# A hybrid decoder layer on one core: shift and squares through PSUM, kept low halves for the input projection, and a place of its own for the last phase's scaled x

## The chip, the core and the metric

The kernel runs on one core of a Trainium2 chip. The metric is device time of one execution in microseconds (us); lower is better. Several executions are timed and their median is given. A separate execution is profiled: its trace tells when each instruction of each engine ran.

The engines have these names in the profile: PE does matrix products (PEld its weight loads), DVE is the vector engine, ACT the scalar engine, POOL the GpSimd engine, SP the engine that issues most DMAs. SBUF and PSUM are the on-chip memories; PSUM receives the matrix products; the kernel divides it into eight banks, m0 to m3, aux0, aux1, cb and dec.

## What is computed

One decoder layer for 1024 prompt rows and 8 sample rows of width 1024, cut to what matters here:

```python
h = x + 0.5 * rmsnorm(swiglu(rmsnorm(x, n_ffn1_pre), gate1, up1, down1), n_ffn1_post)
proj = rmsnorm(h, n_mix_pre) @ w_in                     # 1024 x 3328
q, k, v, pb = ...                                        # attention takes q, k, v; RWKV-7 takes pb
xs = pb + (shifted(pb) - pb) * mu_shift                  # token shift, shifted by one row
r, k, v, xw, xa, xg = split(xs)                          # then decay, delta rule, group norm, gate
h = h + rmsnorm(concat(attention, rwkv) @ w_out, n_mix_post)
h = h + 0.5 * rmsnorm(swiglu(rmsnorm(h, n_ffn2_pre), gate2, up2, down2), n_ffn2_post)
```

The feed-forward blocks have an inner width of 2816. The outputs are h for all rows and the new keys, values, matrix states and shift rows.

## The kernel before

**Tiles and phases.** The rows are cut into two halves: 512 prompt rows with the 8 samples (520 columns), and 512 prompt rows. Activations lie transposed, features on the 128 partitions, rows along the free axis. The stream called trunk does the feed-forward work in four phases: phase 0 and 1 are the first block for the first and the second half, phase 2 and 3 the second block. Phases 0 and 3 use, for most of their gates and ups, a scheme with seven block products in place of eight (`s_combine`, `seven`). Between the phases lie the input projection (stream proj, once per half), the jobs of the RWKV part (four per half), rotary encoding, attention (attn0, attn1), decoding for the samples (dec, decb) and the output projection (out for the first half, outb for the second).

**Precision.** Every float32 product is done as three faster ones: each operand is split into a high part (a rounded copy) and a low part (value minus high part). `split` (L599) does this for weights: a copy on ACT, then a subtraction on DVE or POOL, whichever is free sooner, into one of the buffers w0 to w3. As a weight is used for both halves, the low part may be kept: if `kept` is given, the first use writes the low part to DRAM after it is computed (`aside`, L615) and the second use reads it from there straight into the low half of the buffer, with no subtraction. `LOWS` (L99) names where this is done: the second feed-forward block (1) and w_out ("out"), but not w_in. Which buffer serves which column of w_in is fixed in `s_linear` (L652): columns alternate between two buffers, and a column's buffer is filled once the column before last has been used. `s_project` (L1438) orders the 26 columns of 128 outputs; in the second half 24 of them are computed on all 512 rows at once. A finished column goes to the DRAM tile PT.

**Token shift.** `mixed` (L1627) loads one 128-feature strip of 512 rows, with the row before, from PT into a tile E. It subtracts on POOL and then multiplies by mu_shift and adds on DVE. It is called twice in `s_lora` (L1640) and three times in each of four jobs, per half.

**Norms.** `stats` (L794) takes the sum of squares over eight tiles for a norm: ACT squares a tile, DVE or POOL adds it up. The squares lie in SBUF: in a single buffer "sqs" for the phases 2 and 3 (`s_stats`, L1198), in the two buffers "sq" in the tails of phases 0 and 1 (`s_tail`, L1234). `s_pre` (L1206) makes the split operands x of a phase: multiply by the norm, then scale into the high part on ACT and the low part on DVE. For phase 3 the product with the norm lies in the same two buffers "sq" that the trunk's own sums of squares use.

**What sets the order.** The streams are Python generators that put instructions into per-engine queues. A planner (`run`, L475) walks through time with a cost for each instruction and always issues, per engine, what can start first; among those that can start at the same time it takes the one due first. Due times come from a dry run: `latest` (L564) goes backwards through a planned run and notes for each instruction when it is needed at the latest. `BIAS` (L94) shifts the due times of a stream (trunk2 is the trunk's phase 2, job03 the fourth job of the stream job0, and so on, counted over both halves). `PASSES` (L93) says how many dry runs there are, each with the due times of the one before. The resulting order is written into the program for each engine, SP's DMA queue included, and the engines keep to it: an instruction that waits holds up what is queued behind it on its engine.

**Banks and places.** A stream takes its PSUM banks in turn from a list given with it; the jobs begin on the bank "dec", `s_stats`, `s_pre` and the norms after w_out have the same one, and the tails have "dec" and "aux0". The tile "dreg" (4160 words per partition) is used in turn by the first norm, phase 1's activations, the decoding streams, the second half's attention and the combined blocks of phases 0 and 3.

Of the kernel before, what the change touches and what calls it, by code (L numbers as in the profile page):

```python
# [17 lines left out]
AF = mybir.ActivationFunctionType  # L18
ALU = mybir.AluOpType
# [3 lines left out]
P = 128  # L23
# [6 lines left out]
HS = 512  # L30
# [15 lines left out]
NB = 14  # L46
# [11 lines left out]
def const_table():  # L58
# [11 lines left out]
    for g in range(4):  # L70
        for j in range(8):
# [8 lines left out]
W_DEC = 4160  # L80
# [9 lines left out]
MW = 1  # L90
MARG = 0
SLACK = 0.02
PASSES = 2  # L93
BIAS = {"trunk2": 310, "outn3": -60, "outb0": 30, "pre2": -3, "outn0": -30, "rows0": -30, "job00": -10, "job03": 10, "stats0": 10, "dec0": 10, "wts3": 3, "pre3": -30, "mix1": -60, "lora1": 3, "attn11": 3, "tail2": 3}  # L94
SHIFT = {}
RESAT = 3
GROUPS = {(0, 10): [[0, 1, 2], [3, 4], [5, 6, 7], [8, 9]], (3, 6): [[0, 1, 2], [3], [4, 5]],
          (0, 8): [[0, 1, 2], [3, 4], [5], [6, 7]], (0, 6): [[0, 1, 2], [3], [4, 5]], (3, 4): [[0, 1], [2, 3]], (3, 8): [[0, 1, 2], [3, 4], [5], [6, 7]]}
LOWS = (1, "out")  # L99
STARVE = 1  # L100
HUNGER = 0.1
RB = "dec"
# [25 lines left out]
def col(t):  # L128

    return t + TD * (t >= HS)  # L130
# [79 lines left out]
class Kern:  # L210
# [99 lines left out]
    def put(self, eng, op, fn, a, k):  # L310
# [14 lines left out]
        if o.late is not None:  # L325
            o.late += BIAS.get(st.part, 0) + sum(d for a, b, d in self.shift.get(st.part, ()) if a <= o.key[1] < b)
        self.price(o, op, a, k, outs[0], ins)
# [385 lines left out]
    def columns(self):  # L713

        nc, I = self.nc, self.I
        rows = self.E[:, :P]
        t = self.T(self.const, [P, P], "cols")
        r = 0
        for nm in ("n_ffn1_post", "n_mix_pre", "n_mix_post", "n_ffn2_pre", "n_ffn2_post",
                   "subln", "mu_shift", "w0", "a0", "k_k", "k_a", "r_k", "ln_x_w", "ln_x_b"):  # L720
            a = I[nm]
            if len(a.shape) == 3:
                a = a.rearrange("o h d -> o (h d)")
            k = a.shape[1] // P
            nc.sync.dma_start(rows[r:r + k, :], a[0].rearrange("(k p) -> k p", p=P))
            self.col[nm] = (t, r, k)
            r += k
        yield
        pt = self.ps2()
        nc.tensor.transpose(pt[:, :r], rows[:r], self.ident[:r, :r])  # L730
        nc.vector.tensor_copy(t[:, :r], pt[:, :r])
        for nm, k in (("n_ffn1_post", 0.5), ("n_ffn2_post", 0.5), ("subln", 1.0 - LAM_INIT), ("w0", 0.5), ("a0", 0.5)):
            nc.vector.tensor_scalar(self.vecs(nm), self.vecs(nm), k, None, ALU.mult)
        self.omka = self.T(self.const, [P, 4], "omka")
        nc.vector.tensor_scalar(self.omka, self.vecs("k_a"), -1.0, 1.0, ALU.mult, ALU.add)
        yield
# [57 lines left out]
    def stats(self, src, rb, tmp=("sqs", 1), **kw):  # L794

        for k in range(KT):
            self.square_sum(rb, src[k], k, self.tmp(*tmp, rb.shape[-1]), **kw)
        self.rstd(rb)

    def pair(self, k, src, gain, x):  # L800
# [62 lines left out]
    def s_weights(self):  # L863
# [3 lines left out]
        for ph in range(4):  # L867
# [4 lines left out]
            for n, (kind, f, m0) in enumerate(seq):  # L872
# [26 lines left out]
                kept = None  # L899
                if ph // 2 in LOWS and (kind == "down" or f < FAST[3 * (ph // 2)]):  # L900
                    kept = self.Ld[ph // 2][grp[0]:grp[-1] + 1, :, m0 * P:m0 * P + nm].rearrange("q p m -> p q m") if kind == "down" else \
# [304 lines left out]
    def s_pre(self, ph):  # L1206

        half = ph % 2
        if ph > 1:
            yield ("wait", ("outw", half))  # L1210
        for c, (_, n) in enumerate(CHUNKS[ph]):
            yield ("wait", ("stage", ph, c))
            if ph:
                yield ("wait", ("stats", ph, c))
            if c == 0:
                tiles = self.two(half)
                x = self.x[ph] = self.parts(ph, *tiles)
                self.xt[ph] = [t.rearrange("p (k t) -> p k t", t=520) for t in tiles]
            for k in range(KT):
                src = self.staged[c]  # L1220
                if ph:

                    t = self.tmp("sq", 2, n) if ph == 3 else src[k]
                    self.either("tensor_tensor", t, src[k], self.own[c][2][:, :n], ALU.mult)
                    src = {k: t}
                for step in self.pair(k, src, f"n_ffn{1 + ph // 2}_pre", x[c]):
                    step()
                if k % 4 == 3:
                    yield
            self.signal(("x", ph, c))  # L1230
            yield
        self.signal(("staged", ph))
# [141 lines left out]
    def s_loadx(self, half):  # L1374
# [28 lines left out]
        if half == 0:  # L1403
            yield ("wait", ("loaded", 0, "up", RESAT, None))
        for hf in range(2):
# [32 lines left out]
    def s_project(self, half):  # L1438
# [25 lines left out]
        if half:  # L1464
            units[:4] = [(0, 0), (1, 0), (0, 1), (1, 1)]
        yield from self.linear(("in", half), [self.column(self.I["w_in"], m) for m in ms], units, None, out, places,
                               [(self.Li[m], half == 0) for m in ms] if "in" in LOWS else None)
        self.signal(f"proj{half}")

    def s_out(self, half):  # L1470
# [48 lines left out]
        if half:  # L1519
            yield ("wait", "states")  # L1520
        yield from self.linear(("out", half), src, units, px, out, None, [(self.Lo[i % KT], half == 0) for i in range(len(src))] if "out" in LOWS else None)
        self.signal(("outw", half))
# [16 lines left out]
    def s_mix(self, half):  # L1539

        pool = self.pool
        yield ("wait", "setup")
        for m in (24, 25):
            yield ("wait", ("done", half, m))
        yield ("wait", ("staged", 1 + half))
        self.front = self.stage()
        self.spawn(self.s_lora(pool, half), "lora", 0)
        for i in range(4):
            self.spawn(self.s_job(pool, i, half), f"job{i % 2}", 0, "dec")
        self.sets = []  # L1550
        for j in range(2):
            if half:
                yield ("wait", "proj1")
            self.job_buffers(half, j)
            self.signal(("sets", half, j))
        for what in (f"jobs0_{half}", f"jobs1_{half}", f"rope{half}") + ("dec_b",) * half:
            yield ("wait", what)
        self.a_buffers(pool, half)
        self.spawn(self.s_prepare(pool, half), "prep", 0, "cb")
        for b in range(2):  # L1560
            self.spawn(self.s_attend(pool, half, b), f"attn{b}", 0, f"m{2 + b}", f"aux{b}")
        self.spawn(self.s_finish(pool, half), "fin", 0, "cb")
        if half:
            self.spawn(self.s_states(pool), "states", 2, "cb")
        self.spawn(self.s_out(half), "outb" if half else "out", 0, "m2", "m3")
# [61 lines left out]
    def mixed(self, pool, m, s, out, tag):  # L1627

        nc = self.nc
        t0 = col(s * HS)  # L1630
        E = self.first(tag, 1)
        nc.sync.dma_start(E[:, 1:], self.PT[12 + m][:, t0:t0 + HS])
        if s == 0:
            nc.gpsimd.memset(E[:, 0:1], 0.0)
        else:
            nc.sync.dma_start(E[:, 0:1], self.PT[12 + m][:, HS - 1:HS])
        nc.gpsimd.tensor_tensor(out, E[:, 0:HS], E[:, 1:], ALU.subtract)
        nc.vector.scalar_tensor_tensor(out, out, self.vec("mu_shift", m), E[:, 1:], ALU.mult, ALU.add)

# [297 lines left out]
    def s_decode_a(self):  # L1937
        yield ("wait", "setup")
        yield ("wait", ("staged", 1))
        yield ("wait", ("done", 0, 3))  # L1940
        yield ("wait", "lead")
        yield from self.a_decode()
        self.spawn(self.s_decode_b(), "decb", 1, "dec", ahead=8)

    def s_decode_b(self):
        yield ("wait", "proj0")
        take = self.arena(self.T(self.pool, [P, W_DEC], "dreg"))
        yield from self.b_decode(take, take, take(TD, C))
        self.signal("dec_b")

    def s_states(self, pool):

# [587 lines left out]
def hymba_kernel(ctx, tc, I, O, late=None, dry=False):  # L2540
    K = Kern(ctx, tc, I, O, late, dry)
# [35 lines left out]
    for half in range(2):  # L2577
        K.spawn(K.s_project(half), "proj", 0, "m2", "m3")
        K.spawn(K.s_rope(K.pool, half), "rope", 2)
        K.spawn(K.s_mix(half), "mix", 2)  # L2580
    K.spawn(K.s_decode_a(), "dec", 1, "cb", ahead=24)
    K.run()
    if dry:
        raise Planned(K.predicted, K.latest())
# [40 lines left out]
```

## Time and profile before

| | |
|---|---|
| median of 3 runs | 2302.5 us (2299.95 to 2308.67) |
| profiled execution, its own time | 2294.3 us |
| its span, first to last instruction | 2292.3 us |
| mean granted PE clock | 0.991 |
| moved by DMA | 343.15 MB, mean 150 GB/s |

Nearly all lines in the profile are L317, the helper that records every instruction, so the tiles tell what is what: trunk_m is a product of the trunk in one of its banks, wts_w a split feed-forward weight, lin_w a split weight of w_in or w_out, proj_m a product of the input projection, outb_m one of the second w_out, mix_T and mix_X working tiles of jobs and attention, Lo the DRAM tile of the kept low parts of w_out, Dd a DRAM tile of the decoding. An arrow reads output from inputs. In a row of the timeline the first two numbers are start and length in us, and the bracket at its end gives the engine's idle time before it and what ended that. In a row of a tile's view the three numbers are the shortest, median and longest duration in ns, then the first and last start. In a row of groups the numbers behind the bar are busy time in us and mean ns, then the idle time before and its releasers. In the waits the numbers are us in total, count, and the longest. In the rows of stretches each engine's busy time is followed by its count of instructions.

### The profile page before, as it was taken

Reading aid. Unit: us, or ns where it says so; the run is one execution under the profiler, and the core shown is the slowest. Engines: PE = TensorE matmul, PEld = TensorE weight load, DVE = VectorE, ACT = ScalarE, POOL = GpSimd, SP = SyncE. Lnnn points to the kernel's source line nnn. Section 1 sums busy time; section 2 is a strip of 40 time slices with the busy share of each in tenths; the row PEclk is TensorE's granted clock in tenths of the full one; section 3 lists DMA queues with packets and bytes.
Section 4 is the critical chain, followed back from the end, with each engine's and each line's share of the span. In section 5 each row is a group of like instructions: output and inputs, shape, how many; then the busy total and the mean of one; then the engine's idle time right before and its main releaser. Section 6 shows DMA issues by size and latency. Waiting matters only on the chain. (4 is left out here: it accounts for less than half of the span.)

```text
span 2292.3 us, 42829 instructions
## 1 busy us (share of the span) xinstructions
PE 2228.0 (97%) x15857; PEld 1985.3 (87%) x15857; DVE 1556.5 (68%) x3545; ACT 1078.0 (47%) x2231; POOL 1021.6 (45%) x846
## 2 busy tenths in 40 slices
PE   8999999999999999999899999999999999999998
PEld 7999999799887778988787867777788888999998
DVE  5477988756766687477866367665667356777776
ACT  5433443634354365434552145443665556544444
POOL 3344565534343566356543124333443254544443
PEclk9999999999999999999899999999999999999999
DMA  6423334344334576655679643324745847544543
GB/s 205 132 86 100 102 93 130 104 146 140 109 113 108 170 228 204 218 151 151 194 200 225 169 138 114 111 75 121 205 122 168 273 145 249 148 114 130 148 138 111
DMA packets 476295, 343.15 MB, mean 150 GB/s; under 512 B 82457, under 2 KB 424061, under 8 KB 476088
## 3 DMA queue, kind: packets, MB, share of 16 engines
q1 hardware_dynamic: 475480, 338.82, 50.8%
q8 instruction: 125, 2.05, 0.4%
q0 software_dynamic: 320, 1.08, 0.1%
q14 instruction: 82, 0.67, 0.1%
q10 hardware_dynamic: 288, 0.52, 0.1%
HBM read 278.98 MB, written 61.38 MB: 148 GB/s over the span
## 5 line engine op out<-in xcount | busy, mean ns | idle before, releaser
L317 PE MATMUL trunk_m<-trunk_xl,wts_w 128*128 128x256 f32 (+2 forms) x2700 | 459.4, 321 | 6.9 <-DVE trunk_xl L317 6.2
L317 POOL TENSOR_TENSOR wts_w<-wts_raw,wts_w 128x1024 fp32r<-128x1024 f32 (+2 forms) x162 | 314.4, 1948 | 318.1 <-ACT wts_w L317 279.4
L317 PE MATMUL trunk_m<-pre_X,wts_w 128*128 128x512 f32 (+3 forms) x2400 | 439.9, 335 | 5.7 <-POOL wts_w L317 2.8
L317 PEld LDWEIGHTS trunk_m<-trunk_xl,wts_w 128*128 128x128 f32 x2700 | 382.3, 189 | 42.3 <-DVE trunk_xl L317 7.9
L317 PEld LDWEIGHTS trunk_m<-pre_X,wts_w 128*128 128x128 f32 x2400 | 352.6, 190 | 48.2 <-issue 6.8
L317 PE MATMUL trunk_m<-pre_T,wts_w 128*128 128x512 f32 (+3 forms) x1848 | 362.8, 347 | 5.2 <-DVE trunk_xl L317 2.4
L317 ACT CAST wts_w<-wts_raw 128x1024 fp32r<-128x1024 f32 (+2 forms) x293 | 244.2, 848 | 237.9 <-PE trunk_m L317 162.1
L317 PEld LDWEIGHTS trunk_m<-pre_T,wts_w 128*128 128x128 f32 x1848 | 286.9, 190 | 43.7 <-issue 3.8
L317 DVE TENSOR_TENSOR trunk_xl<-trunk_xl,trunk_m 128x256 f32<-128x256 f32 (+2 forms) x351 | 165.8, 489 | 77.3 <-PE trunk_m L317 76.1
L317 PE MATMUL proj_m<-tail_xl,lin_w 128*128 128x256 f32 (+1 forms) x1248 | 168.5, 290 | 2.3 <-POOL lin_w L317 1.9
L317 PEld LDWEIGHTS proj_m<-tail_xl,lin_w 128*128 128x128 f32 x1248 | 155.6, 190 | 11.3 <-issue 7.0
L317 POOL TENSOR_TENSOR trunk_xl<-trunk_t,trunk_xl 128x512 fp32r<-128x512 f32 (+3 forms) x86 | 94.5, 1100 | 149.9 <-ACT trunk_xl L317 149.7
L317 PE MATMUL proj_m<-tail_T,lin_w 128*128 128x512 f32 (+1 forms) x672 | 153.1, 386 | 4.9 <-ACT tail_T L317 3.8
L317 PEld LDWEIGHTS proj_m<-tail_T,lin_w 128*128 128x128 f32 x672 | 122.6, 192 | 33.2 <-ACT tail_T L317 4.2
L317 DVE TENSOR_TENSOR wts_w<-wts_raw,wts_w 128x1024 fp32r<-128x1024 f32 (+2 forms) x101 | 108.1, 1071 | 35.1 <-ACT wts_w L317 34.4
L317 POOL TENSOR_TENSOR wts_w<-wts_lraw,wts_w 128x512 fp32r<-128x512 f32 x44 | 66.4, 1512 | 53.5 <-ACT wts_w L317 46.9
L317 ACT CAST wts_w<-wts_lraw 128x512 fp32r<-128x512 f32 x94 | 55.9, 617 | 64.7 <-DMA wts_lraw<-in_ffn_down_dram 33.4
L317 POOL TENSOR_TENSOR lin_w<-lin_raw,lin_w 128x1024 fp32r<-128x1024 f32 x19 | 45.9, 2417 | 79.4 <-ACT lin_w L317 69.7
L317 DVE TENSOR_TENSOR trunk_t<-trunk_g,trunk_m 128x512 f32<-128x512 f32 (+2 forms) x75 | 42.1, 562 | 53.4 <-PE trunk_m L317 50.7
L317 POOL TENSOR_TENSOR mix_T<-mix_T 128x512 f32<-128x512 f32 x32 | 38.6, 1207 | 79.2 <-DMA mix_T<-PT 54.6
L317 PE MATMUL trunk_aux<-trunk_xl,wts_w 128*128 128x256 f32 (+1 forms) x516 | 71.5, 283 | 0.0
L317 PE MATMUL trunk_m<-comb_T,wts_w 128*128 128x260 f32 x540 | 69.8, 283 | 0.0
(645 smaller groups left out, 4273.9 us busy)
## 6 DMA issues: line engine op xcount, KB each, us to landing
wts_raw<-in_ffn_gate_dram SPq DMA_DIRECT2D x88, 512.0 KB
wts_raw<-in_ffn_up_dram SPq DMA_DIRECT2D x58, 512.0 KB
wts_raw<-in_ffn_down_dram SPq DMA_DIRECT2D x56, 384.0 KB
wts_raw<-in_ffn_down_dram SPq DMA_DIRECT2D x29, 512.0 KB
lin_raw<-in_w_in_dram SPq DMA_DIRECT2D x26, 512.0 KB
wts_w<-Ld SPq DMA_DIRECT2D x22, 512.0 KB
mix_T<-PT SPq DMA_DIRECT2D x37, 256.0 KB
Ld<-wts_w SPq DMA_DIRECT2D x24, 384.0 KB
```

Source lines behind the costliest of these rows:

```text
L317: o = Op(eng, lambda: fn(*a, **k), st)
```

## The change

It does five things. Token shift (`MIX`): ACT scales the strip by 1 - mu_shift into a PSUM bank, and one DVE instruction multiplies the shifted strip by mu_shift and adds that; POOL has no part in it. The factors 1 - mu_shift are made once in `columns`, and the stream lora is given the bank "dec" for this. Squares (`SQP`): in `stats` the squares after the first go to a PSUM bank and DVE does all sums. Low parts: w_in joins `LOWS`, so its low parts are written to the DRAM tile Li in the first half and read in the second. Phase 3's scaled x: all 16 products lie in the tile "dreg", each in its own columns. Order: `PASSES` is 3 and `BIAS` has other entries. The flag `SWAP` is 0, so what hangs on it (another start of the decoding stream decb) does not take place.

```diff
-PASSES = 2
-BIAS = {"trunk2": 310, "outn3": -60, "outb0": 30, "pre2": -3, "outn0": -30, "rows0": -30, "job00": -10, "job03": 10, "stats0": 10, "dec0": 10, "wts3": 3, "pre3": -30, "mix1": -60, "lora1": 3, "attn11": 3, "tail2": 3}
+PASSES = 3
+BIAS = {"trunk2": 300, "outn3": -60, "outb0": 30, "pre2": -3, "prep1": 3, "job11": 3, "attn11": -10, "job12": 30, "states0": -3}
+SWAP = 0
+MIX = 1
+SQP = 1
-LOWS = (1, "out")
+LOWS = (1, "in", "out")
...
+        self.rest_mu = self.T(self.const, [P, NB], "rmu")
+        nc.vector.tensor_scalar(self.rest_mu, self.vecs("mu_shift"), -1.0, 1.0, ALU.mult, ALU.add)
...
         for k in range(KT):
-            self.square_sum(rb, src[k], k, self.tmp(*tmp, rb.shape[-1]), **kw)
+            if SQP:
+                self.square_sum(rb, src[k], k, self.ps2()[:, :rb.shape[-1]], engines=("vector",))
+            else:
+                self.square_sum(rb, src[k], k, self.tmp(*tmp, rb.shape[-1]), **kw)
...
+                scaled = self.T(self.pool, [P, W_DEC], "dreg") if ph == 3 else None
...
-                    t = self.tmp("sq", 2, n) if ph == 3 else src[k]
+                    t = scaled[:, 2112 * c + n * k:2112 * c + n * k + n] if ph == 3 else src[k]
...
-        self.spawn(self.s_lora(pool, half), "lora", 0)
+        self.spawn(self.s_lora(pool, half), "lora", 0, "dec")
...
+        if MIX:
+            part = self.ps2()
+            nc.scalar.activation(part, E[:, 1:], AF.Copy, scale=self.rest_mu[:, m:m + 1])
+            nc.vector.scalar_tensor_tensor(out, E[:, 0:HS], self.vec("mu_shift", m), part, ALU.mult, ALU.add)
+            return
         nc.gpsimd.tensor_tensor(out, E[:, 0:HS], E[:, 1:], ALU.subtract)
         nc.vector.scalar_tensor_tensor(out, out, self.vec("mu_shift", m), E[:, 1:], ALU.mult, ALU.add)
```

More of the change, by code (lines that the diff above doesn't have):

```diff
@@ L1941, in s_decode_a @@
         yield ("wait", "lead")
+        if SWAP:
+            yield ("wait", "decb")
         yield from self.a_decode()
-        self.spawn(self.s_decode_b(), "decb", 1, "dec", ahead=8)
+        if SWAP:
+            self.signal("dec_b")
+        else:
+            self.spawn(self.s_decode_b(), "decb", 1, "dec", ahead=8)
     def s_decode_b(self):
         yield ("wait", "proj0")
+        if SWAP:
+            yield ("wait", "setup")
+            yield ("wait", "lead")
         take = self.arena(self.T(self.pool, [P, W_DEC], "dreg"))
         yield from self.b_decode(take, take, take(TD, C))
-        self.signal("dec_b")
+        self.signal("decb" if SWAP else "dec_b")
     def s_states(self, pool):
@@ L2581, in hymba_kernel @@
     K.spawn(K.s_decode_a(), "dec", 1, "cb", ahead=24)
+    if SWAP:
+        K.spawn(K.s_decode_b(), "decb", 1, "dec", ahead=8)
     K.run()
```

## The prediction, as put on record before the result

> **What bounds the kernel now.** I read the page first, then the stretches of the run stage by stage.
>
> ```profile
> span 2292.3 us, 42829 instructions
> PE 2228.0 (97%) x15857; PEld 1985.3 (87%) x15857; DVE 1556.5 (68%) x3545; ACT 1078.0 (47%) x2231; POOL 1021.6 (45%) x846
> ```
>
> PE is the bound: it idles for 2292.3 - 2228.0 = 64.3 us in all. The change adds and removes no matrix product, so whatever it gains must come out of these 64.3 us. The busy times by stretch say where they lie. Columns: length, then busy time of PE, PEld, DVE, ACT and POOL, granted clock, DMA share, GB/s.
>
> ```profile
> 0.00:30.00 30.00, 19.31 (x99) 17.00 (x100) 16.04 (x51) 20.16 (x40) 10.74 (x13) 0.89 0.51 157
> 1130.00:1150.00 20.00, 12.13 (x60) 11.28 (x60) 13.52 (x28) 10.56 (x24) 12.39 (x15) 0.66 0.83 259
> 1330.00:1600.00 270.00, 262.03 (x1942) 202.00 (x1942) 184.91 (x557) 131.39 (x274) 97.49 (x69) 1.00 0.42 116
> 1840.00:1930.00 90.00, 80.63 (x545) 75.07 (x546) 52.75 (x94) 48.40 (x88) 42.57 (x51) 0.94 0.52 159
> 1930.00:2270.00 340.00, 340.00 (x2833) 339.95 (x2833) 251.61 (x535) 155.32 (x321) 153.33 (x139) 1.00 0.49 145
> 2270.00:2292.30 22.30, 14.44 (x122) 13.55 (x120) 12.40 (x26) 13.48 (x33) 10.12 (x14) 0.95 0.26 96
> ```
>
> The first 30 us lack 10.7 us of PE and the last 22.3 lack 7.9; nothing in the change reaches these. The long last phase, 1930 to 2270, lacks nothing. That leaves 64.3 - 10.7 - 7.9 = 45.7 us. Of these the change comes near three places: the end of the second phase with the start of the second projection (7.9 in 1130 to 1150), the token jobs beside the third phase (8.0 in 1330 to 1600), and the passage into the last phase (9.4 in 1840 to 1930). So the most that it can win is some 25 us, 1.1%, and each engine's relief counts only where PE waits for that engine.
>
> The profiled execution took 2294.3 us, 2.0 more than its span and 8.2 less than the median of 2302.5. I work out a difference against the 2294.3 and add it to the median.
>
> **Low parts of the second projection.** The first projection still computes the low halves of its weights, and now also writes each (26 writes of 512 KB). The second reads them back instead of computing them. What it stops doing, between 1130 and 1330:
>
> ```profile
> L317 DVE TENSOR_TENSOR lin_w<-lin_lraw,lin_w 128x1024 fp32r<-128x1024 f32 x10 | 12.9, 1287 | 2.7 <-ACT lin_w L317 2.7
> L317 DVE TENSOR_TENSOR lin_w<-lin_LT,lin_w 128x1024 fp32r<-128x1024 f32 x6 | 7.8, 1294 | 1.0 <-ACT lin_w L317 1.0
> L317 POOL TENSOR_TENSOR lin_w<-lin_LT,lin_w 128x1024 fp32r<-128x1024 f32 x7 | 17.1, 2443 | 48.3 <-ACT lin_w L317 46.2 <-DMA decb_dreg<-Dd 2.1
> L317 POOL TENSOR_TENSOR lin_w<-lin_lraw,lin_w 128x1024 fp32r<-128x1024 f32 x2 | 5.1, 2534 | 8.2 <-ACT lin_w L317 8.2
> 1141.14 5.08 PE L317 MATMUL proj_m<-tail_T,lin_w 128*128 128x256 f32 x21 [1.17 <-DVE tail_T L317]
> 1230.26 0.63 PE L317 MATMUL job_dec<-init_ident,mix_T 128*128 128x128 f32 x4 [1.86 <-DVE mix_T L317]
> ```
>
> DVE gets back 12.9 + 7.8 = 20.7 us and POOL 17.1 + 5.1 = 22.2. PE waited there for a crowded DVE once inside the projection, 1.86 us, and 1.17 us before it. I take **-1.9**, between 0 and -3.0.
>
> Against it stand the reads. A column's low half can be fetched only when the column before last has left its weight buffer; the fetch then has the time of one column on PE. The same code path already runs in the second w_out, whose fetches the chain of waits shows (start, length):
>
> ```profile
> 1250.00:1300.00 50.00, 50.00 (x216) 40.22 (x215) 25.27 (x31) 11.35 (x12) 9.92 (x5) 1.00 0.72 189
> 1797.65 6.59 DMA lin_w<-Lo
> 1818.17 6.55 DMA lin_w<-Lo
> 1834.32 7.51 DMA lin_w<-Lo
> PE outb_m L317 <- DMA lin_w<-Lo: 2.6, 3, 2.1
> SPq L317 <- PE outb_m L317: 17.6, 9, 3.4
> ```
>
> A wide projection column is 24 products of 50.00 / 216 = 231 ns, 5.6 us. A fetch of 6.55 to 7.51 us is 1.0 to 1.9 us too long for it; 24 wide columns then cost 24 to 46 us if PE has nothing else. In the second w_out PE had products of the third phase between the columns and lost only 2.6 us over 16 fetches; scaled to 24, that is 3.9. The planner sees such waits coming and can put third-phase products here too. The row of the same code path is nearest: **+3.9**, between 0 and +46. By the Trainium skill, "DMA: Bandwidth & Descriptors", section "Anatomy of one DMA", a transfer costs about 2.0 us plus its bytes over 436 GB/s (a fit stated for the GpSimd path), an estimate of 3.2 us for 512 KB; by it the fetch would fit and the sum would be 3.9 lower, but the 6.55 us above disagree with it under load.
>
> The fetch waits on SP for PE. Queued behind it there are raw weights, result stores and the jobs' loads; SP waited 17.6 us for PE that way in w_out, and a raw weight that slips makes the next column late too. Bandwidth is the other limit:
>
> ```profile
> 1130.00:1140.00 10.00, 3.27 (x11) 2.78 (x11) 7.08 (x15) 4.69 (x10) 5.42 (x7) 0.66 0.94 306
> 1200.00:1330.00 130.00, 127.77 (x556) 101.66 (x554) 65.69 (x95) 27.74 (x31) 33.26 (x18) 1.00 0.73 188
> 1840.00:1850.00 10.00, 8.12 (x52) 7.97 (x53) 3.10 (x5) 3.24 (x7) 2.78 (x4) 0.83 0.98 311
> ```
>
> From 1200 to 1330 the DMA is free for 0.27 x 130 = 35 us; 24 fetches are 12.6 MB, 40 us at the full rate of 311 GB/s. It only just does not fit, which is the ground for the upper end. At 1130 the DMA is at 0.94 and 306 GB/s when the phase's tail waits for its residual; two more fetches of 512 KB ahead of that cost 1.05 MB / 306 = 3.4 us, none if behind: **+1.7**.
>
> The 26 writes fall between 450 and 680. The DMA has room there:
>
> ```profile
> 450.00:680.00 230.00, 225.11 (x2048) 206.68 (x2047) 149.34 (x449) 94.34 (x180) 86.52 (x69) 0.99 0.43 124
> ```
>
> 57% of 230 us is free, and 13.6 MB at 311 GB/s are 44. **0**; without that cover a write is 1.7 us before its weight buffer can be refilled.
>
> **Token shift.** A subtraction on POOL and a multiply-add on DVE become a scaling on ACT into PSUM and a multiply-add on DVE that reads it, 28 times. Nearest rows, the last for a DVE operand in PSUM:
>
> ```profile
> L317 POOL TENSOR_TENSOR mix_T<-mix_T x32: 1035/1043/2037, 481.4 to 1502.9; 128x512 f32<-128x512 f32 x32
> L317 DVE SCALAR_TENSOR_TENSOR mix_T<-mix_T,setup_cols,mix_T x24: 732/746/2905, 483.8 to 1487.1; 128x512 f32<-128x512 f32 x24
> L317 ACT ACTIVATE mix_T<-mix_T,setup_cols 128x512 f32<-128x512 f32 x8 | 5.8, 719 | 9.9 <-DVE mix_T L317 9.9
> 1778.80 0.68 DVE L317 SCALAR_TENSOR_TENSOR trunk_g<-trunk_t,trunk_m 128x512 f32<-128x512 f32 x1
> PE job_dec L317 <- DVE job_hres L317: 4.4, 2, 2.4
> POOL mix_T L317 <- DMA mix_T<-PT: 56.8, 16, 8.0
> ```
>
> One shift goes from 1.04 + 0.75 to 0.72 + 0.68, 0.39 us shorter; 28 make 11 us of the jobs' chains, and ACT gets 20 us more. But between 1330 and 1600 PE lacks only 8.0 us, its other time covered by third-phase products. The largest named wait, 4.4 us, is for DVE work of another job queued ahead. One wait changes its queue: POOL stood 56.8 us, at most 8.0 at a time, until a shift's rows had come from DRAM. ACT now takes that wait, and queued behind it are the casts of weights and the copies out of PSUM that PE waits for; PSUM bank dec, which the jobs' own products use, is held until DVE has read it. ACT is busy 131.39 of 270 us, so the order leaves room. I take **-1.0**, between -4.4 and +8.0, one such wait in full. The 14 complements of the shift factors are one small DVE instruction in the setup, and the branches under SWAP are off: 0.
>
> One row is out of line: the 2905 ns among 746. It ran together with this POOL instruction:
>
> ```profile
> 1215.05 2.44 POOL L317 TENSOR_TENSOR lin_w<-lin_LT,lin_w 128x1024 fp32r<-128x1024 f32 x1
> 1215.13 2.90 DVE L317 SCALAR_TENSOR_TENSOR mix_T<-mix_T,setup_cols,mix_T 128x512 f32<-128x512 f32 x1 [1.49 <-POOL mix_T L317]
> ```
>
> DVE stood until POOL was done, then needed its 0.75. Both edits so far remove such pairs. By the Trainium skill, "SBUF — State Buffer", section "SBUF: two separate sides", DVE with two SBUF inputs and POOL lock each other out for a whole instruction; the trace agrees (2.90 beside 2.44).
>
> **Squares in PSUM, scaled x apart.** In four places (the tails of the first two phases, the norms ahead of the last two) 14 sums of squares each went to POOL or DVE; now all go to DVE with the square in PSUM. The last phase's scaled x takes a place of its own, instead of two buffers shared with the trunk's squares. That place is free: by the first two rows attention last reads it at 1756 and the combined blocks come at 1925.
>
> ```profile
> L317 PE MATMUL attn_aux<-mix_dreg,mix_T x16: 309/351/398, 1622.1 to 1756.0; 128*128 128x320 f32 x4, 128*128 128x384 f32 x4, 128*128 128x448 f32 x4, 128*128 128x512 f32 x4
> L317 ACT CAST comb_dreg<-comb_acc x4: 407/409/411, 1925.2 to 1958.0; 128x260 fp32r<-128x260 f32 x4
> L317 POOL TENSOR_TENSOR bset_bv<-bset_bv,stats_sqs x15: 731/774/1456, 1002.0 to 1884.7; 128x256 f32<-128x256 f32 x9, 128x264 f32<-128x264 f32 x6
> 1874.25 3.19 POOL L317 TENSOR_TENSOR outb_T<-outb_T,outn_hres 128x256 f32<-128x256 f32 x4
> 1877.40 2.34 POOL L317 TENSOR_TENSOR wts_w<-wts_raw,wts_w 128x1024 fp32r<-128x1024 f32 x1
> 1879.79 5.81 PE L317 MATMUL trunk_m<-pre_X,wts_w 128*128 128x256 f32 x34 [2.53 <-POOL wts_w L317]
> 1909.06 4.55 PE L317 MATMUL trunk_m<-trunk_xl,wts_w 128*128 128x256 f32 x35 [1.52 <-DVE trunk_xl L317]
> 1918.20 7.62 PE L317 MATMUL trunk_m<-pre_T,wts_w 128*128 128x264 f32 x48 [1.89 <-ACT trunk_sq L317]
> ```
>
> PE waits 2.53 us for a weight that POOL finishes late, behind residual sums and two sums of squares of 0.77; and 1.89 for a trunk square whose buffer the scaled x shares. I take both, **-4.4**, between 0 and -5.9 with the 1.52.
>
> **Sum.** -1.9 + 3.9 + 1.7 - 1.0 - 4.4 = -1.7 us: the profiled execution would come to 2292.6, the median to 2302.5 - 1.7 = **2300.8**. The changed due times and the third planning pass reorder everything besides; I give them 0 and a bound of +-11, a quarter of the 45.7 us that an order can move. A measurement tells about 0.5% from no change, 11.5 us: the forecast is "the same", its own range 2291 to 2314.
>
> **Rivals.** *The fetches stall the second projection* (slower). From the point where the planner keeps the columns back to back as in 1200 to 1330, each pays 6.55 - 5.6 = 1.0 us: 24 us in place of 3.9, 2321. For it: the DMA is overfull by 5 us there. Against: 2.6 us over 16 fetches in w_out. 0.24. *The freed engines pay at once* (faster): all waits named here go (3.0 + 4.4 + 5.9) with no loss to the fetches, and the clock stays up at 1130, where 0.66 over 12.13 busy us costs 4 more: -17, 2285. For it: DVE and POOL lose 43 us of work there, and the standing seen at 1215 with it. Against: of the 7.9 us at 1130 a row here lays only 1.17 to DVE. 0.26. *The new order decides*: the edits do as said, but gaps appear or vanish elsewhere by 12 or more; 0.05 each way.
>
> **Numbers.** Forecast 0.40, the first rival 0.24, the second 0.26, the order 0.10. Faster 0.26 + 0.05 = 0.31, same 0.40, slower 0.29. The range takes in both rivals with half a bound beyond: 2280 to 2326.
>
> **What would show it.** Right: no subtraction left for lin_w after 1130, fetches from a new DRAM tile of 6 to 7 us, PE waits for them of 2 to 6 us in sum, PE idle near 63. Wrong: PE idle in the second projection above 15 us; or, the other way, the passage into the last phase below 3 us and 1130 to 1150 below 4.

## The result and the profile after

The kernel after takes 2286.2 us (median of 4 runs, 2283.27 to 2289.61); the kernel before took 2301.8 us beside it (4 runs, 2299.95 to 2308.67). The ratio is 0.9935, interval 0.9916 to 0.9955: 15.6 us or 0.65% faster. The forecast was 2300.8 us and "the same"; the time that came is that of the second rival, 2285. It lies inside the whole range (2280 to 2326), below the forecast's own (2291 to 2314).

The profiled execution took 2287.7 us. First its page:

```profile
span 2285.6 us, 42938 instructions
PE 2225.9 (97%) x15857; PEld 1980.1 (87%) x15857; DVE 1501.2 (66%) x3568; ACT 1089.2 (48%) x2239; POOL 959.3 (42%) x792
```

PE does the same 15857 products. Its idle time is 2285.6 - 2225.9 = 59.7 us, 4.6 less than before, and its busy time is 2.1 us less. DVE has lost 55 us of work and POOL 62, and the span shows 6.7 of these 117. The two spans differ by 6.7 us, the medians by 15.6: the profiled execution of before was a quick one, 7.5 us under its median. So stretches of the two profiles can show where time went, but they don't add up to the whole difference.

The same stretches as before, and four more, which are needed below (columns as in the prediction):

```profile
350.00:480.00 130.00, 125.66 (x883) 117.20 (x881) 87.57 (x169) 68.68 (x120) 68.50 (x59) 0.99 0.51 158
480.00:1130.00 650.00, 638.32 (x4484) 546.59 (x4483) 427.29 (x1146) 299.18 (x632) 289.81 (x217) 0.99 0.58 172
1130.00:1150.00 20.00, 18.27 (x142) 17.40 (x142) 15.18 (x31) 16.32 (x26) 14.24 (x14) 1.00 0.92 276
1130.00:1200.00 70.00, 66.67 (x398) 58.45 (x398) 46.52 (x89) 45.47 (x76) 38.37 (x32) 1.00 0.85 265
1200.00:1330.00 130.00, 125.53 (x535) 98.36 (x534) 57.70 (x95) 34.02 (x42) 15.54 (x10) 0.99 1.04 276
1330.00:1600.00 270.00, 267.86 (x1908) 206.53 (x1907) 168.76 (x542) 124.93 (x246) 88.77 (x59) 1.00 0.41 115
1840.00:1930.00 90.00, 81.18 (x622) 75.59 (x621) 57.80 (x112) 60.38 (x113) 47.34 (x63) 0.96 0.76 233
1840.00:2000.00 160.00, 151.18 (x1206) 145.58 (x1205) 105.04 (x211) 95.76 (x193) 78.50 (x97) 0.98 0.67 204
```

In the kernel before, the four stretches that the prediction did not show stand so:

```profile
350.00:480.00 130.00, 121.04 (x817) 111.32 (x816) 94.88 (x156) 64.44 (x117) 69.29 (x65) 0.97 0.41 122
480.00:1130.00 650.00, 643.91 (x4561) 552.50 (x4559) 452.22 (x1137) 298.38 (x630) 316.50 (x240) 1.00 0.54 158
1130.00:1200.00 70.00, 61.80 (x348) 54.11 (x349) 47.84 (x90) 36.46 (x69) 36.26 (x37) 0.90 0.72 207
1840.00:2000.00 160.00, 150.63 (x1129) 145.02 (x1130) 102.08 (x188) 88.36 (x172) 77.08 (x88) 0.97 0.55 169
```

PE gained 9.0 - 4.3 = 4.7 us between 350 and 480 (from the first trunk phase to the second, and the start of the first projection), 8.2 - 3.3 = 4.9 us between 1130 and 1200, and 8.0 - 2.1 = 5.9 us beside the jobs. It lost 5.6 us between 480 and 1130 (6.1 idle before, 11.7 now), so that the first gain was spent again by 1130. It lost 2.2 us in the second projection (2.2 idle before, 4.5 now), where DMA is now full (1.04 for 0.73), and 2.5 between 1600 and 1840 (2.2 and 4.6). So it is chance that the three gains add up to 15.5 us, next to the 15.6 of the medians. The passage into the last phase has not become shorter in idle time (8.8 us for 9.4). How the second projection gets its low halves:

```profile
L320 SPq DMA_DIRECT2D lin_w<-Li x26: 319/599/1842, 1126.5 to 1340.9; - x26
L320 POOL TENSOR_TENSOR lin_w<-lin_raw,lin_w x22: 2361/2393/2992, 444.5 to 653.7; 128x1024 fp32r<-128x1024 f32 x22
L320 DVE TENSOR_TENSOR lin_w<-lin_LT,lin_w x3: 1216/1224/1225, 913.3 to 985.3; 128x1024 fp32r<-128x1024 f32 x3
```

There are 26 fetches between 1126.5 and 1340.9, and the last subtractions for lin_w are those of the first projection and of the first w_out; none is left after 1130. What PE waits for (total, count, longest):

```profile
PE trunk_m L320 <- DVE trunk_xl L320: 5.6, 9, 2.1
PE proj_m L320 <- DMA lin_w<-Li: 4.3, 2, 2.3
PE trunk_m L320 <- POOL wts_w L320: 1.4, 4, 0.8
```

The fetches cost PE two waits and 4.3 us. The chain of waits shows one fetch and the column behind it:

```profile
1239.94 8.02 DMA lin_w<-Li
1248.00 7.38 PE proj_m L320 x24
```

### The profile page after: what moved, and what is told of

Read it like the earlier page. It is cut to its first block, busy times and chain, and to the rows that moved or that the text cites. A ratio compares the mean times of both kernels' runs of the same rounds, so it can differ in the third digit from the quotient of the medians.

```text
span 2285.6 us, 42938 instructions
## 1 busy us (share of the span) xinstructions
PE 2225.9 (97%) x15857; PEld 1980.1 (87%) x15857; DVE 1501.2 (66%) x3568; ACT 1089.2 (48%) x2239; POOL 959.3 (42%) x792
## 3 DMA queue, kind: packets, MB, share of 16 engines
q0 software_dynamic: 320, 1.08, 0.1%
## 4 chain that ended last, share of the span: by engine, by line
PE 62%; DVE 5%; DMA 4%; ACT 2%; issue 1%; SPq 1%; POOL 1%; DVEq 0%; ACTq 0%; POOLq 0%
PE trunk_m L320 35%; PE proj_m L320 7%; PE trunk_aux L320 5%; PE job_aux L320 5%; PE out_m L320 2%; PE attn_m L320 2%; PE outb_m L320 2%; PE attn_aux L320 2%; DMA mix_T<-PT 1%; SPq L320 1%; DVE trunk_xl L320 1%; DVE mix_T L320 1%; PE job_cb L320 1%; PE job_dec L320 1%; DMA lin_w<-Lo 0%
## 5 line engine op out<-in xcount | busy, mean ns | idle before, releaser
L320 POOL TENSOR_TENSOR wts_w<-wts_raw,wts_w 128x1024 fp32r<-128x1024 f32 (+2 forms) x170 | 331.9, 1958 | 468.0 <-ACT wts_w L320 352.6
L320 DVE TENSOR_TENSOR wts_w<-wts_raw,wts_w 128x1024 fp32r<-128x1024 f32 (+2 forms) x93 | 100.4, 1080 | 33.3 <-ACT wts_w L320 32.0
L320 POOL TENSOR_TENSOR lin_w<-lin_raw,lin_w 128x1024 fp32r<-128x1024 f32 x22 | 53.4, 2428 | 104.6 <-ACT lin_w L320 96.7
L320 POOL TENSOR_TENSOR wts_w<-wts_lraw,wts_w 128x512 fp32r<-128x512 f32 x44 | 60.8, 1387 | 45.0 <-ACT wts_w L320 41.8
L320 ACT CAST wts_w<-wts_dec 128x512 fp32r<-128x512 f32 x30 | 17.6, 587 | 107.8 <-DVE wts_dec L320 99.0
```

The source lines that it names most:

```text
L320: o = Op(eng, lambda: fn(*a, **k), st)
```

## The experiments

At first there were two theories: **the edits** bring the gain, whatever the order, or **the order** (the new due times and the third pass) brings it. Every kernel here computes the whole layer, and none is faster than the kernel after. "Own due times" are the shifts and passes that a kernel came with; "plain" means no shifts at all and three passes. The table has the median; the ratio to the kernel before on the same chip (whose median was 2299.2 us for the first four, 2300.5 for the next four and 2301.1 for the last); PE's idle us between 350 and 480 and between 1130 and 1200; and, from 1840 to 2000, PE's products and granted clock. The last columns come from the rows of stretches, as above.

| run | us | ratio | idle 350 | idle 1130 | products | clock |
|---|---|---|---|---|---|---|
| before | 2301.8 | 1 | 9.0 | 8.2 | 1129 | 0.97 |
| after | 2286.2 | 0.9935 [0.9916, 0.9955] | 4.3 | 3.3 | 1206 | 0.98 |
| e1 before, after's due times | 2347.3 | 1.0215 [1.0193, 1.0238] | 10.4 | 8.8 | 1009 | 0.95 |
| e2 after, before's due times | 2319.0 | 1.0092 [1.0078, 1.0106] | 5.4 | 3.2 | 1037 | 0.90 |
| e3 after, no low parts | 2300.3 | 1.0004 [0.9994, 1.0015] | 4.9 | 6.8 | 1197 | 0.97 |
| e4 after, old shift | 2315.0 | 1.0061 [1.0040, 1.0081] | 4.5 | 7.5 | 1080 | 0.95 |
| e5 after, old squares | 2347.9 | 1.0208 [1.0181, 1.0234] | 5.2 | 6.7 | 948 | 0.94 |
| e6 after, no own place | 2299.6 | 0.9989 [0.9972, 1.0006] | 4.1 | 3.6 | 1088 | 0.93 |
| e7 after, plain | 2311.8 | 1.0049 [1.0031, 1.0067] | 4.5 | 4.8 | 996 | 0.90 |
| e8 before, plain | 2324.1 | 1.0103 [1.0077, 1.0129] | 10.2 | 8.2 | 1077 | 0.95 |
| e9 e7, no low parts | 2296.5 | 0.9973 [0.9960, 0.9987] | 4.9 | 4.1 | 1199 | 0.98 |
| e10 e7, old squares | 2333.3 | 1.0134 [1.0116, 1.0151] | 5.0 | 9.5 | 932 | 0.86 |
| e11 e7, no own place | 2315.0 | 1.0057 [1.0044, 1.0070] | 4.7 | 2.7 | 941 | 0.86 |
| e12 after, one due time by 1 us | 2305.1 | 1.0014 [1.0003, 1.0025] | 3.8 | 3.0 | 1024 | 0.90 |

### The order alone, the edits alone

Run e1 is the kernel before with the new due times, e2 the kernel after with the old ones.

```diff
-PASSES = 2
+PASSES = 3
...
```

(and the `BIAS` line of the change; e2 is the same the other way round, in the kernel after)

> The kernel before with only the new due-time shifts and the third planning pass; none of the four edits. The change took 15.6 us off 2301.8. If the order made the gain, this run takes most of it: 2282 to 2292. If the edits made it (freed DVE and POOL, squares, the place for scaled x), the order alone is worth nothing or costs something: 2296 to 2312, with PE idle (span less busy PE) at 62 us or more. The prediction gave the order a bound of 11 us either way.

> The changed kernel with the old due-time shifts and two planning passes: the four edits without the new order. If the edits made the gain: 2280 to 2292. If the order made it: 2297 to 2312. In both cases the fetches of the kept low parts should cost PE some 4 us of waits, as in the changed kernel.

Each half alone is slower than before: e1 by 48 us, e2 by 20. In e1 the page and the longest wait are:

```profile
span 2345.5 us, 42848 instructions
PE 2251.3 (96%) x15857; PEld 1994.6 (85%) x15857; DVE 1570.2 (67%) x3546; ACT 1084.3 (46%) x2235; POOL 1021.8 (44%) x845
```

```profile
PE trunk_m L317 <- DVE trunk_xl L317: 22.3, 10, 7.3
```

Idle time rose from 64.3 to 94.2 us, and for the same 15857 products PE was busy 23 us longer: its mean granted clock was lower (0.983 for 0.991). So both simple theories fall. Each set of shifts helps the kernel that it came with and harms the other.

### No shifts at all

A fairer comparison gives both kernels the same rule.

```diff
-BIAS = {"trunk2": 300, "outn3": -60, "outb0": 30, "pre2": -3, "prep1": 3, "job11": 3, "attn11": -10, "job12": 30, "states0": -3}
+BIAS = {}
```

(e7; e8 is the kernel before with the empty `BIAS` and three passes)

> The changed kernel with no due-time shifts at all, three planning passes. Beside e8 it compares the edits under one and the same rule. Both should be slower than their shifted versions; the shift of 300 us on the trunk's phase 2 holds back work that fills the jobs' waits, so I expect 2300 to 2350. Edits theory: 10 to 20 us below e8. Order theory: within 11 us of e8, either sign.

> The kernel before with no due-time shifts, three planning passes; the pair of e7. 2305 to 2360. Edits theory: 10 to 20 us above e7. Order theory: within 11 us of e7, either sign.

Under the plain rule the edits gain 2324.1 - 2311.8 = 12.3 us, and each kernel's own shifts are worth another 22 to 26. First e7, then e8:

```profile
350.00:480.00 130.00, 125.50 (x891) 117.10 (x891) 87.98 (x172) 68.68 (x120) 68.76 (x59) 1.00 0.52 159
1130.00:1200.00 70.00, 65.15 (x383) 56.33 (x382) 45.78 (x83) 43.17 (x73) 39.68 (x33) 1.00 0.82 255
1840.00:2000.00 160.00, 138.28 (x996) 127.55 (x995) 84.08 (x161) 86.96 (x176) 70.01 (x89) 0.90 0.68 206
```

```profile
350.00:480.00 130.00, 119.76 (x816) 110.40 (x815) 91.81 (x159) 64.30 (x116) 66.96 (x64) 0.97 0.41 123
1130.00:1200.00 70.00, 61.82 (x400) 55.80 (x399) 47.88 (x95) 42.87 (x81) 38.27 (x42) 0.93 0.68 200
1840.00:2000.00 160.00, 138.14 (x1077) 132.48 (x1076) 83.84 (x162) 92.72 (x171) 66.53 (x84) 0.95 0.74 227
```

Here the two parts come apart. In the first two places PE's idle time is 9.3 us with the edits and 18.4 without. With the new due times it is 7.7 (after) against 19.3 (e1), with the old ones 8.6 (e2) against 17.2 (before). Under all three rules the edits are worth 8.5 to 11.6 us of idle time there. In the first place these are two orders and not three: the kernel after and e7 have the same order of products up to 646 us, e1 and e8 up to 627. Between the two places, from 480 to 1130, there is no steady sign: 10.7 us idle with the edits for 11.5 without (plain), 11.7 for 18.5 (new due times), 12.3 for 6.1 (old ones). In the third place, the passage into the last phase, the edits show no such sign: of the six, the kernel after did the most products (1206) and its plain version the fewest (996).

### One due time moved by 1 us

This run sizes the order itself: no work and no operation changes.

```diff
-BIAS = {"trunk2": 300, "outn3": -60, "outb0": 30, "pre2": -3, "prep1": 3, "job11": 3, "attn11": -10, "job12": 30, "states0": -3}
+BIAS = {"trunk2": 300, "outn3": -60, "outb0": 30, "pre2": -3, "prep1": 4, "job11": 3, "attn11": -10, "job12": 30, "states0": -3}
```

> The kernel after with one due-time shift 1 us larger (of the stream prep1, 4 us for 3), which changes no work and no operation, only the order from about three quarters of TensorE's program on. If orders that lie close together have times that lie close together, this stays within 4 us of 2286.2 us. If the planner's order is so sensitive that a nudge throws the time, 2290 to 2320 us, and the losses of the single edits undone (13 to 62 us) then hold a part of that size that is not the edit's own.

It took 2305.1 us, 18.9 more than the kernel after, and the two intervals of the ratio lie apart. Up to 1707 us PE's products come in the same order as in the kernel after, so the first two places test nothing here: their 3.8 and 3.0 us idle, for 4.3 and 3.3, show how far two executions of one order differ. (From e7 to e11, one order up to 1817 us, the second place went from 4.8 to 2.7.) The passage did 182 products fewer, which are 182 / 8.33 = 22 us at the last phase's pace (2250 products in the 270 us from 2000 on); the profiled execution was 8.4 us over its median, so part of the 22 is its own. What happened in it, on PE and on DVE:

```profile
1905.95 6.06 PE L320 MATMUL trunk_m<-pre_T,wts_w 128*128 128x264 f32 x48 [0.99 <-DVE trunk_xl L320]
1917.47 1.09 PE L320 MATMUL last_aux<-init_ident,trunk_xl 128*128 128x128 f32 x4 [5.46 <-DVE trunk_xl L320]
```

```profile
1916.12 0.43 DVE L320 TENSOR_TENSOR trunk_xl<-trunk_xl,last_hres 128x256 f32<-128x256 f32 x1 [2.73 <-DMA last_hres<-res]
```

PE does 48 products of the last phase in one go, then waits 5.46 us for the residual sum of the third phase's tail, whose rows had come late by DMA. After that it has small pieces only (transposes for the tail and for w_out's rows), with a wait before nearly each. The columns of the next view are length, PE's busy time and products, granted clock, DMA share, GB/s:

```profile
1908.00:1912.00 4.00, 4.00 (x34) 1.00 1.04 377
1912.00:1916.00 4.00, 0.01 (x1) 0.99 1.03 283
1916.00:1920.00 4.00, 1.76 (x8) 0.50 0.78 207
1920.00:1924.00 4.00, 3.08 (x13) 0.50 0.75 196
1924.00:1928.00 4.00, 2.60 (x7) 0.50 0.87 257
1928.00:1932.00 4.00, 2.06 (x6) 0.50 0.49 130
1932.00:1936.00 4.00, 2.66 (x12) 0.50 0.49 118
1936.00:1940.00 4.00, 3.33 (x12) 0.53 0.26 80
```

The clock falls to half, and stays there for over 20 us. In the kernel after the products of the same group come in pieces between the tail's transposes, so that PE has something to do while it would wait:

```profile
1911.64 0.41 PE L320 MATMUL last_aux<-init_ident,trunk_xl 128*128 128x128 f32 x1
1911.71 3.54 PE L320 MATMUL trunk_m<-pre_T,wts_w 128*128 128x264 f32 x18
1915.09 0.27 PE L320 MATMUL last_aux<-init_ident,trunk_xl 128*128 128x128 f32 x1
1915.12 1.10 PE L320 MATMUL trunk_m<-pre_T,wts_w 128*128 128x264 f32 x7
```

```profile
1904.00:1908.00 4.00, 1.82 (x10) 0.92 1.05 381
1908.00:1912.00 4.00, 2.38 (x7) 0.50 1.06 281
1912.00:1916.00 4.00, 4.00 (x27) 0.73 0.97 266
1916.00:1920.00 4.00, 4.00 (x36) 1.00 0.49 140
```

There the clock is down for some 7 us and comes back with dense work. So an order can cost about 19 us for reasons that no edit has given it, and the single edits have to be read against that. It is one nudge, and it moves only the last quarter of PE's program; what an order can do ahead of 1707 us it does not show.

### The edits one by one

Each was undone twice, once with the kernel's own due times and once under the plain rule; the token shift once.

**Low parts.**

```diff
-LOWS = (1, "in", "out")
+LOWS = (1, "out")
```

> The changed kernel without the kept low parts of w_in: the second half subtracts again. The fetch theory (the reads cost PE more than the subtractions did) expects a gain of the 4.3 us that PE waits for them: 2280 to 2284. The theory that freeing 43 us of DVE and POOL in the second projection pays expects a loss: 2290 to 2300, with PE waits for DVE between 1130 and 1350 back.

> The kernel after without any due-time shift (2311.8 us, three rounds of planning) and with the first projection reading no kept low parts: it subtracts them on the chip again. If the edits have a worth of their own, whatever the order, this one is the smallest of them: the fetch waits of the projection (3.4 us in the kernel after without shifts) go, some 1 to 5 us of waits for the subtraction come back, 2308 to 2314 us. If each edit pays only through the order made for it, undoing it moves the time in either direction by the size of a new plan, and 2303 or 2320 us is as likely as 2312.

Without them the time rises by 14.1 us with the own due times and falls by 15.3 under the plain rule. The second is below either of the times expected. In e9 the sign is the order's: it gains in the passage, with 1199 products for the 996 of e7,

```profile
1840.00:2000.00 160.00, 151.12 (x1199) 146.98 (x1199) 103.33 (x200) 95.26 (x192) 80.96 (x94) 0.98 0.67 202
```

which lies 500 us behind the projection's last fetch. Both differences are smaller than the 18.9 us of e12, so a price of this edit can't be read from the medians. The stretch of the projection itself tells more. From 1200 to 1330 PE idles 4.5 us with the kept parts and 1.9 without (e3), 3.5 and 1.9 under the plain rule (e7, e9). Without them the wait of job_dec for DVE's mix_T, 1.86 us in the kernel before, is back (1.87 in e3, 0.77 and 1.14 in e9); with them the fetches cost 4.3 and 3.4 us. So in its own stretch the edit loses 1.6 to 2.6 us in both orders. Beside the jobs, from 1330 to 1600, it is the other way: 2.1 us idle with the parts and 9.1 without, 5.5 and 7.5 under the plain rule. From 1130 to 1600 in all that makes 9.9 and 17.8 us with the own due times, 13.8 and 13.5 under the plain rule: a gain that goes with one order.

**Token shift.**

```diff
-MIX = 1
+MIX = 0
```

> The changed kernel with the old token shift (POOL subtracts, DVE multiplies and adds). The prediction priced the edit at -1.0 us, so undoing it alone gives 2285 to 2290. If shorter job chains were what removed 6 us of PE idle between 1330 and 1600, undoing it brings those back: 2291 to 2296. If ACT waiting for a shift's rows costs more than POOL did, it gets faster: below 2282.

It took 28.8 us more; its ten executions spread from 2302.4 to 2326.1 us. But between 1330 and 1600, where the jobs run, PE idles 1.8 us with the old shift and 2.1 with the new one. The time is lost at 1130 to 1200 (7.5 us idle for 3.3) and in the passage (1080 products for 1206), long after the last job (its last product starts at 1633 us). That the shift was to blame for it is not shown.

**Squares.**

```diff
-SQP = 1
+SQP = 0
```

> The changed kernel with the squares of the norms in SBUF again, their sums on DVE or POOL. The prediction gave half of its 4.4 us to this edit (POOL's late weight, 2.5 us). The edits theory expects 2288 to 2292; the order theory expects only what a new order happens to bring, up to 11 us either way, with no PE wait on POOL's sums to show for it.

> The kernel after without any due-time shift (2311.8 us) and with the trunk's squares in their old SBUF buffers, summed by GpSimd or VectorE as the planner has it. If the squares' edit has a worth of its own, the time goes most of the way back to that of the kernel before without shifts (2324.05 us): 2317 to 2326 us, with waits of the product for weights made by GpSimd. If the 62 us that this edit was worth under the kernel's own shifts were all a matter of the order, 2306 to 2315 us.

(The edit is about the squares of the norms, `stats`; the second expectation calls them the trunk's.) Undoing it costs 61.7 us with the own due times and 21.5 under the plain rule, more than was expected and more than all edits together gain there. Both have the same sign, and both exceed e12's 18.9, if the second only just. In both, the stretch from 1130 is worse (by 3.4 and 4.6 us), and PE waits for POOL in the passage: 7.5 us in e5 and 9.4 in e10, where the kernel after has 1.0 and e7 3.5. In e10, on PE, on POOL and in sum:

```profile
1932.38 0.74 POOL L320 TENSOR_TENSOR bset_bv<-bset_bv,stats_sqs 128x264 f32<-128x264 f32 x1 [2.27 <-ACT stats_sqs L320]
1933.87 0.47 PE L320 MATMUL rows_cb<-init_ident,outb_T 128*128 128x128 f32 x1 [3.23 <-POOL outb_T L320]
```

```profile
PE rows_cb L320 <- POOL outb_T L320: 9.4, 8, 4.3
```

POOL does the residual sums after w_out and, between them, sums of squares. The wait of 3.23 us is such a case: POOL stood 2.27 us for a square from ACT, added it up in 0.74, and only then came to the residual sum that PE needed. The longest of these waits, 4.3 us, is not: ahead of it POOL stood idle for DVE. A large part of e5's idle time lies elsewhere, 17.4 us between 1330 and 1600 (2.1 in the kernel after), where no wait for POOL is over 0.7; in e10 it is 7.4 there, for 5.5 in e7. This edit's gain has the same sign in both orders, beyond what e12 moved; one wait shows the edit's own part, and how much of the rest is the order's is open.

**Own place.**

```diff
-                scaled = self.T(self.pool, [P, W_DEC], "dreg") if ph == 3 else None
...
-                    t = scaled[:, 2112 * c + n * k:2112 * c + n * k + n] if ph == 3 else src[k]
+                    t = self.tmp("sq", 2, n) if ph == 3 else src[k]
```

> The changed kernel with phase 3's scaled x back in the two buffers it shares with the trunk's squares. By the prediction PE waits 1.9 us for a trunk square because of that sharing: 2287 to 2291 by the edits theory, and POOL waits for DVE over the scaled x come back (10 us before). If the sharing never held PE, the time is the same within 3 us: 2283 to 2289, and the passage into the last phase lacks as much PE as with it (8.8 us).

> The kernel after without any due-time shift (2311.8 us) and with the last phase's scaled x in the two shared buffers again. If the shared buffers hold up the passage into the last phase whatever the order, one wait of TensorE of 10 to 15 us stands there, for the sums of the trunk's squares, as with the kernel's own shifts (15.3 us), and the time is 2320 to 2327 us. If that wait came of where the own shifts put the scaled x's products, no such wait above 5 us stands there and the time is 2308 to 2315 us.

Up to 1857 us PE's products come in the order of the kernel after, so this is the edit undone that leaves the most of the order as it was. With the own due times it costs 13.4 us, and one wait in e6 is longer than that:

```profile
1921.85 1.22 PE L320 MATMUL last_aux<-trunk_acc,init_onesD 128*128 128x256 f32 x2 [15.28 <-POOL trunk_acc L320]
```

The sums of the trunk's squares end late: on ACT the squares begin when nearly all products of the scaled x (pre_sq) have left the two shared buffers.

```profile
1915.44 0.51 ACT L320 ACTIVATE pre_T<-pre_sq,setup_cols 128x256 fp32r<-128x256 f32 x1 [0.76 <-POOL pre_sq L320]
1916.50 0.42 ACT L320 ACTIVATE trunk_sq<-trunk_xl 128x256 f32<-128x256 f32 x1 [0.55 <-DVE pre_T L320]
```

In the kernel after the same product waits next to nothing:

```profile
1901.18 0.70 PE L320 MATMUL last_aux<-trunk_acc,init_onesD 128*128 128x256 f32 x2 [0.24 <-POOL trunk_acc L320]
```

Under the plain rule there is no such wait in e11; the longest single wait of its passage is another, 3.8 us for a residual sum of POOL (rows_cb waits for outb_T), and the difference in time is 3.2 us.

So the shared buffers are a danger that this order runs into and another does not.

## Why the prediction was right or wrong

**Right: the fetches.** Waits of 3.9 us were taken from the row of the second w_out, with a bound of 46; 4.3 were measured, with third-phase products between the columns as supposed. The fetch in the chain took 8.02 us, a little above the 6 to 7 expected. The first rival (2321 us, columns back to back) did not come: idle time from 1200 to 1330 is 4.5 us, under the mark of 15.

**Right: the subtractions, -1.9.** The wait of 1.86 us for a crowded DVE is gone in the kernel after and back wherever the subtractions are (e3, e9). The other wait counted there, 1.17 us for tail_T, stayed outside the term, as it should: it is 1.6 us now.

**Right: the writes at 0.** Up to 1130 us PE was busy 1101.73 us with them and 1102.65 without (e3), 0.9 us that they may have cost; under the plain rule 1101.26 with and 1098.14 without (e9), which has the other sign.

**Wrong, and small: the residual at 1130, +1.7.** PE's idle time from 1130 to 1150 fell to 1.7 us with DMA at 0.92. Whatever the fetches do to the residual, trunk products cover it, and the clock stays at 1.00 where it was 0.66. The edits are not needed for that: without them, but with other due times, PE idles 0.8 us there (e1) and 0.4 (e8).

**Not told apart: the token shift, -1.0.** The stretch of the jobs is no better with it than without it (2.1 and 1.8 us). What brings the 8.0 us of before back there is undoing the low parts (9.1 us in e3), for which the prediction looked only inside the projection.

**Right in kind, mis-sized: squares and own place, -4.4.** The two waits that the prediction priced are gone: POOL's late weights cost PE 1.4 us in all, 0.8 at the longest, for 2.53 in one, and no product waits for a trunk square. But the price of the shared buffers, 1.89 us, was that of the old order. In the new one it is a wait of 15.28 us (e6). And undoing the squares cost more than the one wait of before showed, 61.7 and 21.5 us, an unknown part of it the order's.

**Missed: 350 to 480.** The prediction named three places that the change comes near; this one, with 9.0 us idle, was not among them. The edits gain 3.5 us there with the old due times and 5.7 to 6.1 in the order that the other two rules share. No single edit undone brings the idle time back (4.1 to 5.2 us). So either more than one of them is enough for it, or it comes of a piece that no run took back (the factors in the setup, the bank given to lora). Which is open. Also missed was the stretch after it, 480 to 1130, where 5.6 us were lost again.

**The step that failed: the order, 0 with a bound of +-11.** The sum gave the changed due times and the third pass nothing, and bounded them by "a quarter of the 45.7 us that an order can move". Both halves of that were wrong. An order can make idle time as well as remove it: e1 has 94.2 us where before had 64.3. And idle time costs twice, as the clock falls: the same 15857 products took PE 2225.9 us in the kernel after, 2238.6 in e12 and 2251.3 in e1, at mean granted clocks of 0.993, 0.989 and 0.983. One due time moved by 1 us gave 18.9 us, the due times of the other kernel 33 (e2, against the kernel after) and 48 (e1). A bound of some +-26 us would have held e12 and both plain kernels against their own; only one of twice that size holds e1. By these runs the 0.05 each way for "the new order decides" was much too little.

So the gain came as the second rival's number and not on its way, and the sum does not explain it: that the time lies in the whole range is luck. Of the second rival's marks one was met (1130 to 1150 below 4 us), which e1 and e8 meet without the edits, and one was not (the passage below 3; it is 8.8). The edits bring some 10 us of idle time in two places under every rule tried, though not all of it lasts (480 to 1130). The due times that came with this kernel keep the passage short: under the plain rule the same edits give 2311.8 us, and with the old due times 2319.0, with 996 and 1037 products in the passage for 1206. **Open:** how the 15.6 us divide between edits and order, since the profiled execution of before was 7.5 us under its median and the stretches explain 6.7; and why these due times serve the passage.

## What to carry to other kernels

In a kernel whose order is fixed by a planner with shifted due times, an edit undone alone measures the edit and a new order together; nudge a due time by a microsecond first, better several times and early in the program too, and trust no single edit whose effect is smaller than what that gives. Compare two kernels also under one rule without shifts, and look for the stretches in which they differ in every order. Where the work of one phase runs out, see to it that the next one's products lie between the tail's small pieces, and give each of the chains there a buffer of its own: a wait there costs its length and then the clock.

## What the runs showed of the hardware

The granted clock fell to 0.50 during a wait of 5.46 us in e12 and stayed there while PE worked in small pieces, busy 44 to 77% of the 4 us slices from 1916 to 1936; it came back near the end of the next slice, which was 83% busy. In the kernel after it fell to 0.50 at about 1907.4 (the slice from 1904 to 1908 has 0.92, so 0.64 us of it were at half) without any long wait: the two longest in that slice ahead of the fall were these.

```profile
1905.02 0.49 PE L320 MATMUL rows_cb<-init_ident,outb_T 128*8 128x128 f32 x3 [1.08 <-ACT rows_X L320]
1907.01 0.74 PE L320 MATMUL rows_cb<-init_ident,outb_T 128*8 128x128 f32 x4 [0.91 <-ACT rows_X L320]
```

PE's busy share of the slice from 1904 to 1908 was 1.82 / 4 = 46%, and the clock was lost; it came back within the slice from 1912 to 1916, in which PE was busy all 4.00 us. The Trainium skill, "TensorE: Matmul & The Clock Gate", section "Part 1: The HAM clock gate (the "warmup" mystery)", says that the clock is halved after about one idle window of 3.4 us and full again after a busy one. The wait in e12 and the return of the clock agree with it; the fall in the kernel after, with no wait over 1.08 us ahead of it, shows that short waits that fill half of the time do it too.
